# Another order for the second part of an output projection and the norms behind it, in a two-layer diffusion trunk

## The chip, the cores and the metric

The kernel runs on one core of a Trainium2 chip. The metric is device time in microseconds (us) for one execution. TensorE (PE in the profile) multiplies matrices; the loads of its stationary operand are the rows marked PEld. VectorE is DVE, ScalarE is ACT, GpSimd is POOL, and SyncE is SP, which issues the DMAs of this kernel. Every engine works through its own instructions in a fixed order.

## The reference

The reference is one inference step of a trunk with two layers. Five blocks of 128 tokens (four of latents, one of context) go through each layer. The part that the change touches is the end of the attention sub-layer and the beginning of the feed-forward one:

```python
o_s = window_attention_latent(rope_2d(q), rope_2d(k), v, ...) @ w_o_a[j]
...
xp = xp + mp[2] * op
xs = xs + ms[2] * o_s
hp = modulate(rmsnorm(xp, norm_ffn_w[i]), mp[3], mp[4])
hs = modulate(rmsnorm(xs, norm_ffn_w[i]), ms[3], ms[4])
...
u = h @ w_up          # first step of conv_ffn: 1024 x 5632
```

The attention output times `w_o` (1024 x 1024), with a gate, is added to x. Each row of x is then normalised, scaled and shifted, and becomes the input of the up-projection. The second layer does the same with `w_o_b`.

## The kernel before

Values are float32, and a product is made of three: each operand is split into a high part (rounded, in the type fp32r) and a low part (value minus high part), and high x high, high x low and low x high are summed. ACT makes the high part (L157 for weights, L389 for the normalised activations), POOL subtracts to get the low part (L160, L390). So a weight tile is a DMA into a staging tile, an ACT copy and a POOL subtraction.

Half of the output projection's sum is done during attention (`o_first`, tile `ps_op`). `finish_layer` runs the second half, once per layer, and then the feed-forward part. The words of one string give its order:

```python
OPROJ = "00 10 20 01 11 21 n0 30 n1 40 w0 n2 31 41 w1 u0 n3d w2 u1 n4d u2 u0 u1 u2"
```

- `th`, as `31`: `product` for token block t and column half h (512 columns). Four k steps, 18 matmuls into `ps_dn` (two buffers). DVE multiplies by the gate (L476, which frees the buffer) and adds to x (L477, both inputs in SBUF). With h = 1 it also starts `norm_stat`: ACT squares the row of x and sums (L352), a few small DVE and ACT steps make the reciprocal root (L299 to L306), and DVE scales the row into `xn` (L353). The weights of a column half are three pieces of 768, 768 and 512 columns.
- `nt`: `norm`: eight PE transposes of `xn` (L138, `ps_nt`), then `norm_post`: per half of four 128-blocks, scale and shift on DVE (L379, first half) or ACT (L381, second half), the high part on ACT (L389, tiles `hF_00` and `hF_01`), the low part on POOL (L390, tiles `hF_10` and `hF_11`).
- `wi`: load of an up-projection weight tile (128 columns of `w_up`) in two pieces of 768 and 256 columns. The 768 pieces, and the 256 of w0, are staged in `ust`, the other two in `wst`. High and low parts lie in six rotating pairs of buffers (`w_bufs` = 6), which the six pieces of the output projection hold before them: w0 takes the two pairs of the first column half's first pieces, w1 that half's third and the second column half's first, w2 the second half's other two. A piece can be written once the last product that reads its pair is through with it.
- `ui`: half of an up product: 320 columns, that is token blocks 0, 1 and half of 2 in the first half, the rest in the second. It has 24 matmuls; the first twelve read `hF_00` and `hF_10`, the last twelve `hF_01` and `hF_11`.

Behind these words two more up tiles are loaded ahead (`wx`, 1024 columns each, staged in a second `ust` tile that can be filled only when PE has read `oh` and `ol`, the split attention output, for the last time, in product 41).

PE's order is the order of the words (`chain` in `mm` and `tr`). On the other engines and the DMA queue a scheduler fixes the order of the instructions when the kernel is built; nothing is reordered at run time.

Of the kernel before, what the change touches and what calls it, by code (L numbers as in the profile page):

```python
# [51 lines left out]

LAST = "40a 41a 00a 01a 40b 41b 00b 01b 10 11 n4 20 n0 21 30 n1 31 n2 q6 n3"

OPROJ = "00 10 20 01 11 21 n0 30 n1 40 w0 n2 31 41 w1 u0 n3d w2 u1 n4d u2 u0 u1 u2"


def _f(ap):
# [1127 lines left out]
def finish_layer(k, l, wo, of, xsrc, cw):  # L1186
    nc = k.nc
    with ExitStack() as c:
# [39 lines left out]
        ust = k.ap.tile([P, 4 * T], F32, name="ust", tag="act")  # L1228
        for c_ in OPROJ.split():
            i = int(c_[1])  # L1230
# [158 lines left out]
```

## Time and profile before

| | |
|---|---|
| median of 3 runs | 1721.25 us (1717.64 to 1725.33) |
| profiled execution | 1718.12 us, of which the span from first to last instruction is 1716.3 us |
| PE busy | 94% of the span |
| PEld, DVE, ACT, POOL busy | 85%, 50%, 45%, 55% |
| mean granted TensorE clock | 0.981 of full speed |

PE is busy nearly all the time, so its idle times and its slow stretches are what can be won or lost. The words of `OPROJ` run from about 362 to 425 us in layer 0, and again, with the same pattern, from about 1212 to 1274 us in layer 1.

### The profile page before, as it was taken

What the parts mean: (1) busy time and instruction counts of PE and PEld (TensorE: products, weight loads), DVE (VectorE), ACT (ScalarE), POOL (GpSimd) and SP (SyncE); (2) the same over time, 40 slices, a digit from 0 to 9 for tenths busy, and PEclk for the clock granted to TensorE, in tenths of its full rate; (3) what the DMA queues carried; (4) which work ended last, traced back from release to release, by engine and by line L of the source; (5) the groups of instructions that cost most, each with busy time, mean ns of one, the idle gap of its engine ahead of it and who ended that gap; (6) DMA issues with size and microseconds to landing.
All of it is one profiled execution on the core that took longest, in us unless ns stands there. A gap on an engine that the chain in (4) does not pass through costs nothing. (4 is left out here: it accounts for less than half of the span.)

```text
span 1716.3 us, 26311 instructions
## 1 busy us (share of the span) xinstructions
PE 1619.1 (94%) x9736; PEld 1453.7 (85%) x9736; DVE 862.6 (50%) x2109; ACT 771.5 (45%) x1719; POOL 939.4 (55%) x786
## 2 busy tenths in 40 slices
PE   6789989999999999999969999998999999999998
PEld 4557767678999999999868899987899999999997
DVE  5766676765323243233555667677643333332334
ACT  4556566536323233223446777776452323323131
POOL 1434345447565675656336766776365647646461
PEclk9899999999999999999989999999999999999999
DMA  8455465561322222222122211223522212213131
GB/s 315 148 204 183 181 224 205 191 222 52 97 70 78 74 86 74 74 74 73 63 87 77 70 53 50 61 94 118 168 86 75 86 62 87 86 50 99 50 99 62
DMA packets 74592, 184.86 MB, mean 108 GB/s; under 512 B 16200, under 2 KB 25672, under 8 KB 74464
## 3 DMA queue, kind: packets, MB, share of 16 engines
q1 hardware_dynamic: 74464, 183.18, 32.0%
q8 instruction: 77, 1.26, 0.3%
q14 instruction: 51, 0.42, 0.1%
HBM read 171.32 MB, written 14.12 MB: 108 GB/s over the span
## 5 line engine op out<-in xcount | busy, mean ns | idle before, releaser
L132 PE MATMUL ps_up<-hF,whi 128*128 128x320 f32 x2688 | 598.6, 310 | 5.4 <-POOL hF L390 5.4
L160 POOL TENSOR_TENSOR wlo<-wst,whi 128x1024 fp32r<-128x1024 f32 (+3 forms) x190 | 417.1, 2199 | 218.8 <-ACT whi L157 218.5
L132 PEld LDWEIGHTS ps_up<-hF,whi 128*128 128x128 f32 x2688 | 454.8, 189 | 12.6 <-POOL hF L390 6.0
L132 PE MATMUL ps_up<-hF,wlo 128*128 128x320 f32 x1344 | 415.3, 310 | 0.0
L157 ACT ACTIVATE whi<-wst 128x1024 fp32r<-128x1024 f32 (+3 forms) x195 | 186.7, 962 | 415.1 <-PE ps_dn L132 158.0
L936 DVE SCALAR_TENSOR_TENSOR z<-ps_up,convc,z 128x511 f32<-128x511 f32 (+1 forms) x176 | 96.0, 545 | 331.1 <-ACT z L934 331.1
L132 PEld LDWEIGHTS ps_up<-hF,wlo 128*128 128x128 f32 x1344 | 253.1, 189 | 1.7
L477 POOL TENSOR_TENSOR x<-x,xtmp 128x512 f32<-128x512 f32 x100 | 128.8, 1293 | 143.1 <-DVE xtmp L476 143.0
L476 DVE TENSOR_TENSOR xtmp<-ps_dn,gate 128x512 f32<-128x512 f32 x120 | 81.9, 690 | 244.5 <-PE ps_dn L132 244.5
L132 PE MATMUL ps_mm<-whi,hB 128*128 128x384 f32 x580 | 181.3, 351 | 9.3 <-DVE rs_r L341 8.5
L132 PE MATMUL ps_dn<-whi,gh 128*128 128x512 f32 x440 | 172.8, 393 | 1.7 <-DVE xtmp L476 1.6
L132 PE MATMUL ps_dn<-wlo,gh 128*128 128x512 f32 x440 | 172.3, 392 | 0.0
L132 PE MATMUL ps_dn<-whi,gl 128*128 128x512 f32 x440 | 169.8, 389 | 0.0
L132 PE MATMUL ps_mm<-whi,hA 128*128 128x384 f32 x320 | 111.0, 376 | 8.3 <-ACT hA L268 6.3
L132 PEld LDWEIGHTS ps_mm<-whi,hB 128*128 128x128 f32 x580 | 108.7, 190 | 11.5 <-ACT vb L527 8.9
L961 POOL TENSOR_TENSOR gl<-z,gh 128x640 fp32r<-128x640 f32 x44 | 69.3, 1575 | 81.9 <-ACT gh L960 81.9
L937 DVE SCALAR_TENSOR_TENSOR z<-ps_up,convc,z 128x511 f32<-128x511 f32 (+1 forms) x176 | 96.8, 550 | 6.1
L132 PE MATMUL ps_mm<-wlo,hB 128*128 128x384 f32 x290 | 98.6, 340 | 0.0
L132 PEld LDWEIGHTS ps_dn<-whi,gh 128*128 128x128 f32 x440 | 82.6, 188 | 17.9 <-DVE xtmp L476 3.4
L934 ACT ACTIVATE z<-ps_up,convc 128x640 f32<-128x640 f32 x88 | 77.0, 875 | 45.7 <-PE ps_up L132 45.6
L132 PEld LDWEIGHTS ps_dn<-whi,gl 128*128 128x128 f32 x440 | 82.2, 188 | 17.2
L132 PEld LDWEIGHTS ps_dn<-wlo,gh 128*128 128x128 f32 x440 | 82.6, 188 | 13.6
(214 smaller groups left out, 2919.4 us busy)
## 6 DMA issues: line engine op xcount, KB each, us to landing
adst<-in_wada_dram SPq DMA_DIRECT2D x96, 512.0 KB, 6.1
wst<-in_wup_dram SPq DMA_DIRECT2D x78, 512.0 KB, 3.4
wst<-in_wdown_dram SPq DMA_DIRECT2D x44, 512.0 KB, 3.4
wst<-in_wqb_dram SPq DMA_DIRECT2D x29, 384.0 KB, 3.2
wst<-in_wqa_dram SPq DMA_DIRECT2D x16, 384.0 KB, 6.9
xd<-xring SPq DMA_DIRECT2D x20, 256.0 KB, 6.3
x<-xd SPq DMA_DIRECT2D x10, 512.0 KB, 5.6
wst<-in_woa_dram SPq DMA_DIRECT2D x8, 384.0 KB, 5.7
```

The lines of the kernel that those rows point to most:

```text
L132: i = self.nc.tensor.matmul(out, lhsT, rhs, start=start, stop=stop)
L157: i = nc.scalar.activation(hi, st, AF.Copy)
L160: (lo_eng or nc.gpsimd).tensor_tensor(lo, st, _f(hi), OP.subtract)
L476: nc.vector.tensor_tensor(tmp, ps, gate[:, j, sl], OP.mult)
L477: (nc.gpsimd if pool_add else nc.vector).tensor_tensor(x[:, sl], x[:, sl], tmp, OP.add)
L934: nc.scalar.activation(z, u, AF.Identity, scale=w[:, 1:2], bias=w[:, 3:4])
L936: nc.vector.scalar_tensor_tensor(z[:, a + 1:b], u[:, a:b - 1], w[:, 0:1], z[:, a + 1:b], op0=OP.mult, op1=OP.add)
L937: nc.vector.scalar_tensor_tensor(z[:, a:b - 1], u[:, a + 1:b], w[:, 2:3], z[:, a:b - 1], op0=OP.mult, op1=OP.add)
L961: nc.gpsimd.tensor_tensor(gl[:, k], zz[0], _f(gh[:, k]), OP.subtract)
```

## The change

One string is another. The same words stand in another order, and no instruction is added or removed.

```diff
-OPROJ = "00 10 20 01 11 21 n0 30 n1 40 w0 n2 31 41 w1 u0 n3d w2 u1 n4d u2 u0 u1 u2"
+OPROJ = "00 10 20 30 40 w0 01 11 21 n0 31 n1 41 n2 w1 u0 n3d w2 u1 n4d u2 u0 u1 u2"
```

All five first column halves come first. The first up weights w0 are loaded right behind them. Then come the second halves, with n0, n1 and n2 behind 21, 31 and 41. Before, products 31 and 41 stood between n2 and u0; now n2 stands right before u0.

On PE, at the end of the projection in layer 0, before (`oh`, `ol` are the attention output, `ps_nt` the transposes of a norm, `ps_up` the up product u0):

```order
L132 MATMUL ps_dn_4325<-whi_4006,ol_3971 128x512
L132 MATMUL ps_dn_4325<-whi_4012,oh_3970 128x512
L132 MATMUL ps_dn_4325<-wlo_4013,oh_3970 128x512
L132 MATMUL ps_dn_4325<-whi_4012,ol_3971 128x512
L132 MATMUL ps_up_4369<-hF0_00_4018,whi_4261 128x320
L132 MATMUL ps_up_4369<-hF0_10_4020,whi_4261 128x320
```

and now:

```order
L132 MATMUL ps_dn_4304<-whi_4012,oh_3970 128x512
L132 MATMUL ps_dn_4304<-wlo_4013,oh_3970 128x512
L132 MATMUL ps_dn_4304<-whi_4012,ol_3971 128x512
L138 MATMUL ps_nt_4337<-ident_72,xn_4215 128x128 x8
L132 MATMUL ps_up_4369<-hF0_00_4018,whi_4120 128x320
L132 MATMUL ps_up_4369<-hF0_10_4020,whi_4120 128x320
```

The transposes of token 2 (`xn_4215`) have moved from two products ahead of u0 to directly ahead of it.

On POOL, in the same place, before. `xn_4134` is token 1 and `xn_4167` token 2; `wlo_4262`, `wlo_4267` are w0, `wlo_4359`, `wlo_4364` w1, `wlo_4417`, `wlo_4422` w2, and `wx` the two tiles loaded ahead:

```order
L390 TENSOR_TENSOR hF0_10_4020<-xn_4134,hF0_00_4018 128x4x128
L160 TENSOR_TENSOR wlo_4262<-ust_4024,whi_4261 128x768
L160 TENSOR_TENSOR wlo_4267<-ust_4024,whi_4266 128x256
L390 TENSOR_TENSOR hF0_11_4021<-xn_4134,hF0_01_4019 128x4x128
L160 TENSOR_TENSOR wlo_4359<-ust_4024,whi_4358 128x768
L390 TENSOR_TENSOR hF0_10_4020<-xn_4167,hF0_00_4018 128x4x128
L160 TENSOR_TENSOR wlo_4364<-wst_4365,whi_4363 128x256
L390 TENSOR_TENSOR hF0_11_4021<-xn_4167,hF0_01_4019 128x4x128
L160 TENSOR_TENSOR wlo_4417<-ust_4024,whi_4416 128x768
L160 TENSOR_TENSOR wlo_4422<-wst_4423,whi_4421 128x256
L160 TENSOR_TENSOR wx_4572<-ust_4571,wx_4572 128x1024
L160 TENSOR_TENSOR wx_4576<-ust_4571,wx_4576 128x1024
```

and now, with `xn_4182` for token 1 and `xn_4215` for token 2 (w0 and the first piece of w1 stand ahead of these rows and of token 0):

```order
L160 TENSOR_TENSOR wlo_4364<-wst_4365,whi_4363 128x256
L390 TENSOR_TENSOR hF0_10_4020<-xn_4182,hF0_00_4018 128x4x128
L160 TENSOR_TENSOR wlo_4417<-ust_4024,whi_4416 128x768
L160 TENSOR_TENSOR wlo_4422<-wst_4423,whi_4421 128x256
L390 TENSOR_TENSOR hF0_11_4021<-xn_4182,hF0_01_4019 128x4x128
L160 TENSOR_TENSOR wx_4572<-ust_4571,wx_4572 128x1024
L390 TENSOR_TENSOR hF0_10_4020<-xn_4215,hF0_00_4018 128x4x128
L160 TENSOR_TENSOR wx_4576<-ust_4571,wx_4576 128x1024
L390 TENSOR_TENSOR hF0_11_4021<-xn_4215,hF0_01_4019 128x4x128
```

Both pieces of w2 and the first `wx` tile have moved from behind token 2 to ahead of its first low part, and the second `wx` tile to between its two.

On ACT, now, from the second piece of w1 on (`xn_4269` and `x_3966` are token 3):

```order
L157 ACTIVATE whi_4363<-wst_4365 128x256
L389 ACTIVATE hF0_00_4018<-xn_4182 128x4x128
L381 ACTIVATE xn_4182<-ps_nt_4283,mcol0_83,abA01_3943 128x128 x2
L352 ACTIVATE xn_4269,nss_4270<-x_3966 128x1024
L381 ACTIVATE xn_4182<-ps_nt_4283,mcol0_83,abA01_3943 128x128 x2
L157 ACTIVATE whi_4416<-ust_4024 128x768
L157 ACTIVATE whi_4421<-wst_4423 128x256
L300 ACTIVATE rs_l_4273<-rs_a_4272 128x1
L389 ACTIVATE hF0_01_4019<-xn_4182 128x4x128
L157 ACTIVATE wx_4572<-ust_4571 128x1024
L389 ACTIVATE hF0_00_4018<-xn_4215 128x4x128
```

The first of these rows writes a buffer that product 41 reads in its first two k steps, and the whole of token 1's split stands behind it; before, token 1's first high part stood three weight pieces earlier.

## Rows read from the trace of the kernel before

**Rows 1.** The page: busy us of each engine, share of the span, instructions
```profile
PE 1619.1 (94%) x9736; PEld 1453.7 (85%) x9736; DVE 862.6 (50%) x2109; ACT 771.5 (45%) x1719; POOL 939.4 (55%) x786
```

**Rows 2.** PE's waits: engine, line, releaser: us in total, times, longest; last row 415-850 us
```profile
PE ps_up L132 <- POOL hF L390: 5.4, 2, 2.7
...
PE ps_dn L132 <- DVE xtmp L476: 0.8, 1, 0.8
```

**Rows 3.** PE in order of time: start, duration, line, operation, tiles [idle before, releaser]
```profile
379.73 1.09 PE L138 MATMUL ps_nt<-ident,xn 128*128 128x128 f32 x8 [0.22 <-DVE xn L353]
...
387.14 0.40 PE L132 MATMUL ps_dn<-whi,ol 128*128 128x512 f32 x1
...
388.72 0.48 PE L132 MATMUL ps_dn<-whi,oh 128*128 128x512 f32 x1
...
394.39 0.30 PE L132 MATMUL ps_up<-hF,whi 128*128 128x320 f32 x1
397.38 0.64 PE L132 MATMUL ps_up<-hF,whi 128*128 128x320 f32 x1 [2.69 <-POOL hF L390]
...
400.48 0.56 PE L132 MATMUL ps_up<-hF,whi 128*128 128x320 f32 x2
...
402.34 1.03 PE L138 MATMUL ps_nt<-ident,xn 128*128 128x128 f32 x8
```

**Rows 4.** Windows: stretch, us, busy time of each engine, granted clock, DMA share, GB/s
```profile
397.40:400.50 3.10, 3.10 (x12) 3.10 (x13) 2.25 (x6) 2.42 (x6) 3.10 (x3) 0.50 0.37 152
```

**Rows 5.** POOL in order of time, layer 0, from the first norm on
```profile
383.21 1.49 POOL L390 TENSOR_TENSOR hF<-xn,hF 128x512 fp32r<-128x512 f32 x1 [10.66 <-ACT hF L389]
...
389.58 2.56 POOL L160 TENSOR_TENSOR wlo<-ust,whi 128x768 fp32r<-128x768 f32 x2 [0.64 <-ACT whi L157]
392.09 1.32 POOL L390 TENSOR_TENSOR hF<-xn,hF 128x512 fp32r<-128x512 f32 x1
...
395.61 1.72 POOL L390 TENSOR_TENSOR hF<-xn,hF 128x512 fp32r<-128x512 f32 x1
397.28 0.73 POOL L160 TENSOR_TENSOR wlo<-wst,whi 128x256 fp32r<-128x256 f32 x1
397.97 1.28 POOL L390 TENSOR_TENSOR hF<-xn,hF 128x512 fp32r<-128x512 f32 x1
399.21 2.28 POOL L160 TENSOR_TENSOR wlo<-ust,whi 128x768 fp32r<-128x768 f32 x1
...
402.59 4.75 POOL L160 TENSOR_TENSOR wx<-ust,wx 128x1024 fp32r<-128x1024 f32 x2
```

**Rows 6.** ACT in order of time, layer 0, around product 41
```profile
391.47 1.51 ACT L381 ACTIVATE xn<-ps_nt,mcol,abA 128x128 f32<-128x128 f32 x4
392.89 0.42 ACT L157 ACTIVATE whi<-wst 128x256 fp32r<-128x256 f32 x1
393.21 0.61 ACT L389 ACTIVATE hF<-xn 128x512 fp32r<-128x512 f32 x1
394.03 1.06 ACT L352 ACTIVATE xn<-x 128x1024 f32<-128x1024 f32 x1 [0.20 <-issue]
...
395.09 0.83 ACT L157 ACTIVATE whi<-ust 128x768 fp32r<-128x768 f32 x1
...
397.99 1.06 ACT L157 ACTIVATE wx<-ust 128x1024 fp32r<-128x1024 f32 x1 [0.47 <-DMA ust<-in_wup_dram]
```

**Rows 7.** DVE in order of time, layer 0: additions to x
```profile
366.38 0.69 DVE L477 TENSOR_TENSOR x<-x,xtmp 128x512 f32<-128x512 f32 x1
...
388.44 1.05 DVE L477 TENSOR_TENSOR x<-x,xtmp 128x512 f32<-128x512 f32 x1
...
392.54 1.42 DVE L477 TENSOR_TENSOR x<-x,xtmp 128x512 f32<-128x512 f32 x1
```

**Rows 8.** DMA issues (SP queue) in order of time: the last load of x, layer 0
```profile
369.93 0.32 SPq L1203 DMA_DIRECT2D x<-xd  x1
```

**Rows 9.** The page, DMA issues: tiles, count, KB each, median us to landing
```profile
x<-xd SPq DMA_DIRECT2D x10, 512.0 KB, 5.6
```

## The prediction

> **What bounds the kernel.** Read the busy times first: PE is busy for 1619.1 us, 94% of the span [rows 1], so a change of order can only win or lose PE's idle times and its slow stretches. Then read PE's waits. In the stretch of the change the wait of an up product for POOL stands out: 5.4 us, once per layer, 2.7 each [rows 2]. PE's instructions in order of time show it. u0's first matmul follows the last product at 394.39, and its second starts only at 397.38, when POOL has written the first low part of token 2 [rows 3]. The windows show a second price: 12 matmuls take the 3.10 us from 397.40 on, at a granted clock of 0.50, which is 1.2 of 2.4 GHz, right after that wait [rows 4]. At full clock 12 take 1.86 (400.48 to 402.34) [rows 3]. So u0's first half lasts from 394.39 to 402.34, 7.95 us, where 24 matmuls at full clock need 3.72: a loss of 4.23 us per layer, of 2.99 waiting and 1.24 clock. That is what a better order could win here, about 8.5 in two layers. Behind u0 PE has a single wait of 0.8 up to 850 us [rows 2], so time lost at u0 isn't caught up later: it is added to the end.
>
> The third view is POOL in order of time. It gets to token 2's first low part at 395.61 because two pieces of w0 (2.56) and the first of w1 lie ahead of it; w2 (2.28 for its first piece, which is as large as w1's) and the two tiles loaded ahead (4.75) come behind it [rows 5]. So the question is what lies between n2 and u0 on POOL after the change, and the rows of the new order answer it.
>
> **The change, part by part,** for layer 0; T is the time at which the last product ends (394.39 before).
>
> *The n2 slot.* n2's transposes leave the row of products. From the start of 40's last matmul plus one spacing (387.14 + 0.23) to 31's first (388.72) they took 1.35 us [rows 3]; T comes earlier by that, and the transposes run inside the wait that follows. Gain 1.35.
>
> *ACT.* The high part of w1's second piece writes a buffer that product 41 reads in its first two k steps. Before, it ran at 392.89, 1.50 ahead of T [rows 6]. In the new row token 1's split, token 3's square and w2's first piece stand behind it. The piece, one high part, the square and the 768 piece ran from 392.89 to 395.92, which is 3.03; the four scale steps add 1.42 (391.47 to 392.89) [rows 6]. So w2's first high part is ready at T - 1.50 + 4.45 = T + 2.95. The bounds are T + 2.0, if the buffer comes free a microsecond earlier, and T + 4, if ACT also waits for DVE's half of token 1.
>
> *POOL.* From there it has w2's first piece 2.28, the second 0.73, token 1's second part 1.28, a `wx` tile 2.38 (half of 4.75), and only then token 2's first part, 1.28 [rows 5]: 7.95 in all. u0's second matmul can start at T + 10.9, where it was T + 2.99. The second `wx` tile and token 2's second part follow, 3.66, so the thirteenth matmul can't start before T + 14.55.
>
> *u0.* After so long without work I take the first 12 matmuls at the half clock, 3.10 [rows 4], to T + 14.0. They then wait 0.55 for the second part, and 12 at full clock end at T + 16.4. Before, it was T + 7.95. The loss is 8.45, less the slot's 1.35: 7.1 us.
>
> *Earlier weights.* w0 and w1's first piece (2.56 and about 2.28 us of POOL, 4.84) now run under the products 01 and 11, where POOL stood idle: it waited 10.66 ahead of 383.21 [rows 5]. They cost nothing there, except through DVE. An addition to x alone takes 0.69; the one at 392.54 beside POOL took 1.42 [rows 7]. It ended at 393.96, 0.55 after the POOL instruction of 392.09 [rows 5]. Now 40's and 01's additions meet these pieces, and 01's starts the chain of token 0's norm, for which PE already waits 0.22 [rows 3]. An addition 0.73 later moves n0 by less, since the norm's next DVE step is queued behind the next product's gate: I take 0.4, between 0 and 2.3 (a whole piece). The Trainium skill (SBUF — State Buffer, "Who interferes with whom") says that a DVE instruction with two SBUF inputs and a GpSimd instruction that reads SBUF exclude each other, and that the later one waits for the whole of the other. The rows agree. By the rule at its worst, 01's addition waits out a whole 2.3 us piece: 1.9 more per layer, and a time of 1740 in place of the one below.
>
> *DMAs.* Four loads into `ust` now come ahead of the last loads of x. The last was issued at 369.93 [rows 8] and its first addition was at 388.44 [rows 7]. Now product 40 comes three products (2.83 each, half of 388.72 to 394.39 [rows 3]) and two norms (1.35 each) earlier, so it adds at about 377.2, 7.3 after that issue, where a load takes 5.6 [rows 9]. I take 0, with an upper bound of 1 us. The second `ust` is still loaded at T; before, ACT copied from it 3.6 us after T (397.99) [rows 6]. Now ACT gets there at about T + 4.2 and POOL at T + 7.2, so 0.
>
> *Everything behind u0* stands in the old order: n3, u1, n4, u2. Their inputs have the same distances or longer ones. Cost 0; it is covered by u1 and u2, and if tokens 3 and 4 came late, u0's second half would wait.
>
> **Sum.** 7.1 + 0.4 = 7.5 us per layer. Layer 1 has the same words, the same new rows on POOL, and the same wait before [rows 2]: 15 in all. Against the profiled execution of 1718.1 that gives 1733.1. The median of the runs shown is 3.1 above it; 15 on the median, 1721.25, gives **1736**. Bounds per layer: about 5.5 (ACT a microsecond earlier, no DVE loss, half of the second part's delay hidden) and 11 (ACT a microsecond later, the second 12 matmuls at half clock too for 1.24, a DVE loss of 1.5): 1732 to 1743.
>
> **Rivals.**
>
> 1. *POOL is free in time, and it isn't slower.* If token 2's first part found POOL idle, only n2's own chain would show. From n0's transposes at 379.73 to the end of its first low part at 384.70 took 4.97 [rows 3, 5]. u0's second matmul would start at T + 5.0, not T + 2.99; less the 1.35 that is + 0.65 per layer: 1722.5. The earlier weights speak for it, since 4.84 us leave POOL's way; the order speaks against it, which puts w2 and a `wx` tile, 5.4 us, in the way instead. It decides whether that low part begins by T + 3.7.
> 2. *A gain.* Were u0 not to wait at all, 8.5 would be won: 1712.8. But 4.97 us from n2 to its low part is longer than the 2.99 that PE waited, so this needs a shorter norm chain than any row shows.
> 3. *Clock and contention add up.* If all 24 matmuls of u0 run at 1.2 GHz and DVE and POOL hold each other up twice more, 10 to 11 per layer: 1742. For it: PE would be idle about three times as long as before. Against: the clock came back within 3.1 us of work.
> 4. *The change acts in one layer only*: + 7.5, 1728.8. The rows of both layers are the same, so this is nearly ruled out.
>
> **How the numbers follow.** A measurement of this kernel can tell about 0.5%, 8.6 us, from no change. The forecast (0.73) and rival 3 (0.13) are slower by more than that: 0.86. Rivals 1 (0.08) and 4 (0.03) lie within it: 0.11. Rival 2 has 0.03. The range of 1727 to 1743 holds the forecast's bounds, with a few microseconds below for the spread of the runs, and the lower half of rival 3; it leaves out rivals 1 and 2.
>
> **What would show it.** In the profile after, PE should wait at `ps_up` for POOL twice in each layer, about 9 to 10 us first and up to 2 at the thirteenth matmul, in place of 2.7 once; POOL's low part of token 2 should start 9 to 10 us after the last product; and the granted clock should be 0.50 for about 3 us from there. The products before should run without gaps, but for about 0.6 at n0. If the low part comes within 5 us of T, the forecast is wrong at the ACT or POOL step; if PE's waits are as said and the time isn't longer, it is wrong in that lost time adds to the end.

## The result and the profile after

The changed kernel takes 1735.14 us (median of 6 runs, 1732.97 to 1739.72), the kernel before 1719.45 on the same chip (6 runs, 1716.58 to 1725.33): 15.7 us more, a ratio of 1.0087 with a 95% interval of 1.0070 to 1.0104. The forecast was 15 more, 1736.

The profiled execution of the change took 1739.72. Its first product starts at 368.7, where it is 362.6 in the one of before. Up to there the instructions are the same, and of the change nothing but the first loads of up weights has been issued: the 6.1 us are spread between executions (in the fourteen profiles of this document that product starts anywhere from 360.4 to 368.7). So stretches are compared here, and not whole spans. I take the stretch of the words from PE's first product (`ps_dn`) to its first matmul with a tile loaded ahead (`wx`). PE's instructions by tile (count, duration in ns, first and last start), layer 0, before:

```profile
L132 PE MATMUL ps_dn<-whi,oh x50: 277/389/496, 362.6 to 393.7; 128*128 128x512 f32 x30, 128*128 128x256 f32 x20
L132 PE MATMUL ps_up<-hF,wx x96: 309/309/309, 421.8 to 435.7; 128*128 128x320 f32 x96
```

and after:

```profile
L132 PE MATMUL ps_dn<-whi,oh x50: 277/389/504, 368.7 to 398.3; 128*128 128x512 f32 x30, 128*128 128x256 f32 x20
L132 PE MATMUL ps_up<-hF,wx x96: 309/309/309, 435.4 to 449.4; 128*128 128x320 f32 x96
```

The words take 59.2 before and 66.7 after: 7.5 more. In layer 1 they take 59.1 (1211.8 to 1270.9) and 66.5 (1225.8 to 1292.3): 7.4 more. From layer 0's words to layer 1's it is 790.0 and 790.4. So 14.9 of the 15.7 lie where the change was made, in both layers.

The page, busy us and instructions, for [rows 1]:

```profile
PE 1625.7 (94%) x9736; PEld 1458.9 (84%) x9736; DVE 865.9 (50%) x2109; ACT 771.8 (44%) x1719; POOL 937.8 (54%) x786
```

PE's 6.6 us more of busy time say little of the change: the instructions are the same, 3.8 of the 6.6 lie ahead of the first product, and only 1.7 in the two stretches of the words. PE's waits, for [rows 2]; the last line is that of 415 to 870 us:

```profile
PE ps_up L132 <- POOL hF L390: 10.2, 4, 4.8
PE ps_up L132 <- ACT hF L389: 8.1, 2, 4.2
PE ps_nt L138 <- DVE xn L353: 7.4, 5, 3.4
...
PE ps_dn L132 <- DVE xtmp L476: 0.8, 1, 0.8
```

5.4 of waiting at `ps_up` have become 18.3. `xn` waits stand as before (7.2 there), and the later stretch has the same single wait of 0.8. PE in order of time, for [rows 3]:

```profile
391.42 1.09 PE L138 MATMUL ps_nt<-ident,xn 128*128 128x128 f32 x8 [0.21 <-DVE xn L353]
...
398.81 0.39 PE L132 MATMUL ps_dn<-whi,ol 128*128 128x512 f32 x1
399.71 1.10 PE L138 MATMUL ps_nt<-ident,xn 128*128 128x128 f32 x8 [0.52 <-DVE xn L353]
404.66 0.64 PE L132 MATMUL ps_up<-hF,whi 128*128 128x320 f32 x1 [3.85 <-ACT hF L389]
410.11 0.63 PE L132 MATMUL ps_up<-hF,whi 128*128 128x320 f32 x1 [4.81 <-POOL hF L390]
...
413.20 0.47 PE L132 MATMUL ps_up<-hF,whi 128*128 128x320 f32 x1
414.12 0.56 PE L132 MATMUL ps_up<-hF,whi 128*128 128x320 f32 x1 [0.45 <-POOL hF L390]
...
415.98 1.03 PE L138 MATMUL ps_nt<-ident,xn 128*128 128x128 f32 x8
```

T, the end of the last product, is 398.81 + 0.23 = 399.04. From the second matmul of u0 (410.11) to the thirteenth (413.20) it is 3.10 us. The window of these matmuls, for [rows 4], has a clock of 0.50 again:

```profile
410.10:413.20 3.10, 3.09 (x11) 3.10 (x12) 2.72 (x2) 0.00 (x0) 3.10 (x2) 0.50 0.00 0
```

POOL, for [rows 5]: w0 and w1's first piece early, then w2, token 1's second part, a `wx` tile, token 2's first part, the other `wx` tile and token 2's second part.

```profile
382.14 4.80 POOL L160 TENSOR_TENSOR wlo<-ust,whi 128x768 fp32r<-128x768 f32 x3 [0.67 <-ACT whi L157]
...
402.36 1.81 POOL L160 TENSOR_TENSOR wlo<-ust,whi 128x768 fp32r<-128x768 f32 x1 [1.55 <-ACT whi L157]
...
404.80 1.28 POOL L390 TENSOR_TENSOR hF<-xn,hF 128x512 fp32r<-128x512 f32 x1
406.02 2.36 POOL L160 TENSOR_TENSOR wx<-ust,wx 128x1024 fp32r<-128x1024 f32 x1
408.33 1.72 POOL L390 TENSOR_TENSOR hF<-xn,hF 128x512 fp32r<-128x512 f32 x1
410.01 2.36 POOL L160 TENSOR_TENSOR wx<-ust,wx 128x1024 fp32r<-128x1024 f32 x1
412.34 1.73 POOL L390 TENSOR_TENSOR hF<-xn,hF 128x512 fp32r<-128x512 f32 x1
```

ACT, for [rows 6]: w2's first high part, and token 2's first one, which u0's first matmul reads:

```profile
401.38 0.84 ACT L157 ACTIVATE whi<-ust 128x768 fp32r<-128x768 f32 x1
...
403.98 0.63 ACT L389 ACTIVATE hF<-xn 128x512 fp32r<-128x512 f32 x1
```

DVE, for [rows 7]: the additions of products 40 and 01, beside POOL's early weights (382.14 to 386.94), are longer, as forecast, but by 0.4 at most, and the one that follows them has the 0.69 of an undisturbed one:

```profile
383.63 0.90 DVE L477 TENSOR_TENSOR x<-x,xtmp 128x512 f32<-128x512 f32 x1
...
386.41 1.08 DVE L477 TENSOR_TENSOR x<-x,xtmp 128x512 f32<-128x512 f32 x1
...
389.19 0.69 DVE L477 TENSOR_TENSOR x<-x,xtmp 128x512 f32<-128x512 f32 x1
```

The last load of x, for [rows 8], is issued at 378.81, and the fifth addition is at 383.63: a margin of 4.8, not the 7.3 of the forecast, because the load is now issued 10.1 behind the first product, where it was 7.3 [rows 8]. No wait shows there.

### The profile page after: what moved, and what is told of

Same layout as the page of the kernel before. It is cut to its first block, busy times and chain, and to the rows that moved or that the text cites. A ratio compares the mean times of both kernels' runs of the same rounds, so it can differ in the third digit from the quotient of the medians.

```text
span 1737.6 us, 26308 instructions
## 1 busy us (share of the span) xinstructions
PE 1625.7 (94%) x9736; PEld 1458.9 (84%) x9736; DVE 865.9 (50%) x2109; ACT 771.8 (44%) x1719; POOL 937.8 (54%) x786
## 5 line engine op out<-in xcount | busy, mean ns | idle before, releaser
L132 PE MATMUL ps_up<-hF,whi 128*128 128x320 f32 x2688 | 600.1, 310 | 18.3 <-POOL hF L390 10.2
L132 PEld LDWEIGHTS ps_up<-hF,whi 128*128 128x128 f32 x2688 | 455.1, 189 | 26.7 <-POOL hF L390 11.7
L132 PEld LDWEIGHTS ps_dn<-wlo,gh 128*128 128x128 f32 x440 | 82.7, 188 | 13.6
```

The lines of the kernel that those rows point to most:

```text
L132: i = self.nc.tensor.matmul(out, lhsT, rhs, start=start, stop=stop)
```

## The experiments

Three helpers serve them. `lo_eng=nc.vector` makes a low part on DVE. `pin_lo` puts a low part's subtraction behind the instruction that stands before it in the program on its engine. `after` puts a weight's high and low part behind two given instructions of ACT and POOL, in the queue alone and without a wait. `post[t]` are token t's last high and low part, `stat[t]` is its reciprocal root's last step on ACT (L303). The cuts of code show the lines that use them; those that define them and hand them on are left out, and `...` marks a place left out between two lines.

All results in one table: words of each layer; both layers together against before; the time between the layers' words (790.0 before); the median against that of before on the same chip; the ratio's interval.

| run | words 0 | words 1 | both | between | median | interval |
|---|---|---|---|---|---|---|
| before | 59.2 | 59.1 | | 790.0 | | |
| the change | 66.7 | 66.5 | +14.9 | 790.4 | +15.7 | 1.0070 to 1.0104 |
| e1_pool_order | 65.2 | 66.1 | +13.0 | 789.5 | +13.1 | 1.0065 to 1.0098 |
| e2_wx_behind | 63.0 | 63.6 | +8.3 | 792.1 | +9.2 | 1.0039 to 1.0076 |
| e3_n2_earlier | 61.3 | 64.8 | +7.8 | 792.0 | +8.6 | 1.0040 to 1.0070 |
| e4_before_pool_order | 63.2 | 62.8 | +7.7 | 790.7 | +9.8 | 1.0046 to 1.0076 |
| e5_t2_low_on_dve | 67.2 | 67.2 | +16.1 | 789.4 | +16.9 | 1.0089 to 1.0115 |
| e6_before_w1_on_dve | 58.5 | 58.3 | -1.5 | 791.7 | +0.8 | 1.0001 to 1.0018 |
| e7_before_t2_low_on_dve | 63.3 | 63.2 | +8.2 | 786.7 | +5.6 | 1.0029 to 1.0058 |
| e8_before_w1_behind_t2 | 59.2 | 59.0 | -0.1 | 788.3 | +0.7 | 0.9989 to 1.0011 |
| e9_t2_first_everywhere | 61.9 | 61.9 | +5.5 | 791.3 | +5.9 | 1.0034 to 1.0069 |
| e10_before_chains_first | 56.2 | 56.1 | -6.0 | 790.2 | -6.2 | 0.9953 to 0.9977 |
| e11_late_w0 | 73.7 | 73.8 | +29.2 | 789.5 | +29.3 | 1.0136 to 1.0199 |
| e12_before_wx_and_w1_behind | 60.3 | 60.0 | +2.0 | 792.3 | +5.3 | 1.0015 to 1.0040 |

The time between the words moves by -3.3 to +2.3 in runs where the build put the second layer's attention in another order (e2, e3, e6, e7, e9 and e12 among them). Part of that is spread: in e8, whose order there is nearly that of before, it moved by -1.7. The verdicts below go by the words.

**What stands ahead of token 2 on POOL.**

```diff
-            k.norm_post(k.norm_tr(xn, t, dn=where == "d"), xn, l, 1, t, hT)
+            k.norm_post(k.norm_tr(xn, t, dn=where == "d"), xn, l, 1, t, hT, pin=False, pin_lo=t == 2)
...
-                ups.append(k.up(hT, [k.load_w(src[:, a:b], b - a, k.wp, None, s)
+                ups.append(k.up(hT, [k.load_w(src[:, a:b], b - a, k.wp, None, s, False, i == 2)
...
-                                  ust[:, 1024 * i:1024 * i + 1024]))
+                                  ust[:, 1024 * i:1024 * i + 1024], False, True))
```

The last argument of `load_w` is `pin_lo`.

> The changed kernel with POOL's order alone altered: both low parts of token 2 stand ahead of w2 and of the two wx tiles, directly behind token 1's second low part. PE's, DVE's and SP's order in these places stays, ACT's but for one square. T is the end of the last product. Theory (what is queued on POOL ahead of token 2 makes the loss): token 2's first high part is ready at about T + 5.6 as in the changed kernel, so its low part ends at about T + 6.9 and u0's second matmul starts there instead of at T + 11.1. Twelve matmuls at half clock end at T + 10.1, the second low part is done by about T + 9.9, and u0's first half ends at about T + 11.9 instead of T + 16.9: 5 us less per layer, 10 in all, about 1725. Rival 1 (n2's own chain directly ahead of u0 is the loss and POOL stands by): PE waits for ACT instead and the time stays between 1732 and 1736. Rival 2 (the loss comes from the column order and the early weights, which hold up DVE): the same, 1732 to 1736, with later starts of n0 to n2.

PE in order of time in this run, layer 0:

```profile
402.39 0.63 PE L132 MATMUL ps_up<-hF,whi 128*128 128x320 f32 x1 [0.93 <-POOL hF L390]
406.38 0.64 PE L132 MATMUL ps_up<-hF,whi 128*128 128x320 f32 x1 [0.42 <-POOL hF L390]
408.93 1.04 PE L138 MATMUL ps_nt<-ident,xn 128*128 128x128 f32 x8
...
416.46 0.42 PE L132 MATMUL ps_up<-hF,wlo 128*128 128x320 f32 x1 [1.80 <-POOL wlo L160]
```

POOL's wait fell from 4.81 to 0.93, as forecast, but u2 then waited 1.80 for w2, which the pin had put behind token 3 as well. u0's first half won 3.4 in layer 0, where 5 were expected, since it also waited 0.42 for token 2's second low part and went on at the lower clock behind that. The words kept 1.5, and 0.4 in layer 1. So the expectation failed by what is late next.

The second run drops the pin on w2:

```diff
-                ups.append(k.up(hT, [k.load_w(src[:, a:b], b - a, k.wp, None, s, False, i == 2)
+                ups.append(k.up(hT, [k.load_w(src[:, a:b], b - a, k.wp, None, s)
```

> The changed kernel with the POOL subtractions of the two wx tiles behind token 2's low parts; w2 stays ahead of them. Theory: token 2's first low part follows token 1's second one at about T + 7.0, and u0's second matmul starts at T + 8.4 instead of T + 11.1; no wait at the thirteenth; u0's first half ends at T + 13.4: 3.5 us less per layer, 7 in all, about 1728. Together with the run in which w2 goes behind too this gives the shares of wx and w2. Rivals 1 and 2: 1732 to 1736. The build also puts ACT's and DVE's instructions of the second layer's attention in another order, which may move the total by some microseconds; layer 0 is read from its own rows.

```profile
405.36 0.63 PE L132 MATMUL ps_up<-hF,whi 128*128 128x320 f32 x1 [2.06 <-POOL hF L390]
```

3.7 and 2.9 us less than the change, where 3.5 were expected, without a new wait: the two `wx` tiles are wanted only behind the words, and their place ahead of token 2 was 39 to 49% of the loss.

**n2's place.**

```diff
-OPROJ = "00 10 20 30 40 w0 01 11 21 n0 31 n1 41 n2 w1 u0 n3d w2 u1 n4d u2 u0 u1 u2"
+OPROJ = "00 10 20 30 40 w0 01 11 21 n0 31 n1 n2 41 w1 u0 n3d w2 u1 n4d u2 u0 u1 u2"
```

> The changed kernel with n2 one product earlier, ahead of product 41: first column halves first and w0 early, as in the change, but a product between n2 and u0. Theory: token 2's low part is now second on POOL only to token 1's; n2 waits up to 1.5 for its norm, u0's second matmul waits 1 to 2.5, and about half of the first twelve matmuls run at half clock: near the time of the kernel before, 1716 to 1724. Rival 1 (n2's place is the loss) says the same, so the run of POOL's order decides between these two. Rival 2 (column order and early weights are the loss): 1730 to 1736, since both are still there.

```profile
396.52 1.97 PE L138 MATMUL ps_nt<-ident,xn 128*128 128x128 f32 x8 [3.15 <-DVE xn L353]
```

u0's first half no longer waits in layer 0, but n2 does, 3.15 for its own norm, and its transposes run at the lower clock (1.97 against 1.09). u0's second half waits 0.88. In layer 1 u0 waits 2.60 and n4 1.55 besides n2. The time lies between the two expectations. The column order and the early weights alone don't cost the 14.9 (against rival 2), but n2's wait was put at half of what it is: n0, 31 and n1 between 21 and n2 are shorter than its chain by 3 us.

**Early weights, undone.**

```diff
-OPROJ = "00 10 20 30 40 w0 01 11 21 n0 31 n1 41 n2 w1 u0 n3d w2 u1 n4d u2 u0 u1 u2"
+OPROJ = "00 10 20 30 40 01 11 21 n0 31 n1 w0 41 n2 w1 u0 n3d w2 u1 n4d u2 u0 u1 u2"
```

> The changed kernel with one part undone: w0 is loaded late again (behind n1 instead of behind the first column halves); the column order and n2's place stay. The prediction took the early weights at no cost, and as 4.84 us that leave POOL's way. Theory: these pieces now stand on ACT (2.5 us) and POOL (w0 2.56 and w1's first piece 2.28) between token 1 and token 2. POOL runs w0, w1, token 1's second half and w2 in a row from about T + 2.5 on, so token 2's first low part ends at about T + 13.6 instead of T + 11; its second one, behind both wx tiles, at T + 19.7 instead of T + 15.1. u0's first half ends at T + 21.6 to T + 22.8 instead of T + 16.9: 4.7 to 5.9 more per layer, 1744 to 1747. Rival (the early weights help nothing, or cost DVE what they save POOL): within 2 per layer of the changed kernel, 1731 to 1739.

```profile
401.44 0.63 PE L132 MATMUL ps_up<-hF,whi 128*128 128x320 f32 x1 [5.15 <-ACT hF L389]
408.29 0.64 PE L132 MATMUL ps_up<-hF,whi 128*128 128x320 f32 x1 [6.22 <-POOL hF L390]
414.58 0.64 PE L132 MATMUL ps_up<-hF,whi 128*128 128x320 f32 x1 [2.73 <-POOL hF L390]
```

7.0 and 7.3 more per layer than the change, above the 4.7 to 5.9 expected. The second matmul came where it was expected (at T + 13.6), but the rest of u0's first half and n3's transposes then ran at the lower clock (0.50 in the windows 408.3 to 411.4 and 414.6 to 417.7). So the change has two parts of opposite sign: the column order with n2 at the end costs 14.5 and 14.7 per layer, and the early weights give 7 of it back.

**DVE instead of POOL.** Token 2's low parts on DVE, in the change (e5) and in the kernel before (e7); w1's in the kernel before (e6):

```diff
-            k.norm_post(k.norm_tr(xn, t, dn=where == "d"), xn, l, 1, t, hT)
+            k.norm_post(k.norm_tr(xn, t, dn=where == "d"), xn, l, 1, t, hT, lo_eng=nc.vector if t == 2 else None)
...
-                ups.append(k.up(hT, [k.load_w(src[:, a:b], b - a, k.wp, None, s)
+                ups.append(k.up(hT, [k.load_w(src[:, a:b], b - a, k.wp, nc.vector if i == 1 else None, s)
```

> The changed kernel with both low parts of token 2 made by DVE instead of POOL; w2 and the wx tiles keep their places on POOL, so nothing is pushed behind. Theory (token 2's low part lost its time in POOL's queue, and the run of POOL's order gave the gain back because w2 then came 2 us too late for u2): the high part is ready at T + 5.6, DVE makes the low part by T + 6.5 to T + 8, u0's first half ends at T + 11.5 to T + 13 instead of T + 16.9, and there is no wait for w2. DVE's two more instructions delay tokens 3 and 4 by up to 1.5. Gain 3 to 5 per layer: 1725 to 1729. Rival (in this stretch any order pays the same, since the sum of the work bounds it): 1732 to 1736.

DVE in order of time in e5:

```profile
398.73 0.76 DVE L390 TENSOR_TENSOR hF<-xn,hF 128x512 fp32r<-128x512 f32 x1 [1.95 <-ACT hF L389]
...
401.04 2.48 DVE L353 TENSOR_SCALAR xn<-x,rs_r 128x1024 f32<-128x1024 f32 x1
403.44 2.82 DVE L390 TENSOR_TENSOR hF<-xn,hF 128x512 fp32r<-128x512 f32 x1
```

and POOL:

```profile
400.58 5.13 POOL L160 TENSOR_TENSOR wx<-ust,wx 128x1024 fp32r<-128x1024 f32 x2
```

PE's first wait for a low part fell to 0.25: that part came in time, but the second one stood behind token 3's scaling, and both were held while POOL split the `wx` tiles: 2.82 for what takes 0.76 alone. PE waited 3.24 at the fourteenth matmul and ran all of u0's first half and n3's transposes at a clock of 0.50. The words take 0.5 and 0.7 more than in the change: nothing of the 3 to 5 per layer was won.

> The kernel before with the low parts of w1 made by DVE. On POOL token 2's low parts then follow token 1's second one directly. Theory: u0's second matmul waits 0.3 to 0.5 instead of 2.7 and at full clock: 3.1 to 4 less per layer, as in the run of the kernel before with POOL's order altered; w1 and w2 are early, so u1 and u2 don't wait. DVE has 1.5 us more to do ahead of the last additions to x, and POOL may hold it up: n3 and n4 wait 1.2 to 2.5. Net gain 1 to 2.5 per layer: 1715 to 1718. Rival (what POOL gives up DVE pays in full, n3 later by as much as u0 is earlier): 1719 to 1722.

> The kernel before with token 2's low parts made by DVE. They stand on DVE behind the gates of the last two products and ahead of additions to x. Theory: u0's second matmul starts within 0.5 of its first, 4 less per layer; token 3's addition comes 0.7 to 1.5 later, so n3 waits 1.5 to 2.5: net 1.5 to 2.5 per layer, 1715 to 1718. Rival: n3 and n4 wait 4 in all, 1720 and more. The build also orders the second layer's attention anew, which cost 2 us in two runs that had the same.

In e6 u0's wait fell to 1.17, and n3 then waited 1.41 and n4 0.49. The words won 0.7 and 0.8 per layer, and the stretch between them, whose attention the build had put in another order, was 1.7 longer (791.7); the net is the rival's. In e7 u0 waited 1.04, at its fourteenth matmul, but n3 5.66:

```profile
406.61 1.94 PE L138 MATMUL ps_nt<-ident,xn 128*128 128x128 f32 x8 [5.66 <-DVE xn L353]
```

Both expectations were too high by what tokens 3 and 4 lose.

**POOL's order in the kernel before.** The pins of e1, with `pin_lo=i >= 1` on the weights (e4) or `i == 1` (e8), and none on `wx`:

> The kernel before with POOL's order alone altered: both low parts of token 2 ahead of w1's first piece (and w2 behind token 3). Theory: token 2's first high part is ready at 391.6 in the trace of before, so its low part can run from 393.35, when token 1's second ends, to 394.7; u0's second matmul starts 0.3 after its first instead of 2.99, at full clock, and the second low part ends before the thirteenth. Of the 4.23 per layer about 4 are won, 8 in all: about 1711.5. Rival: the clock falls at u0 whether PE waits or not, or w1 then comes late for u1: only 2.7 or less per layer, 1714 to 1719.

```profile
413.47 0.63 PE L132 MATMUL ps_up<-hF,wlo 128*128 128x320 f32 x1 [2.74 <-POOL wlo L160]
```

u0's wait fell to 0.45, and its first half ended 3.7 earlier; n3 waited 1.22, and u2 waited 2.74 for w2, with the lower clock behind it. 4.0 and 3.7 more per layer in all: the pins had put w2 behind token 3 again.

> The kernel before with one exchange on POOL: w1's first piece goes behind token 2's two low parts, and nothing else (w2 and the wx tiles keep their places; ACT and SP are the same). It is the run of POOL's order on the kernel before without the 2.7 us wait for w2 and the half clock behind it, which cost 6 there. Theory: u0 3.1 earlier, n3 1.2 and n4 0.5 later, as seen there: 1.4 less per layer, 3 in all, about 1717. Rival (what is put behind always comes late: w1 for u1): u1 waits for wlo for 1 to 3, no gain, 1720 to 1725.

PE in order of time in e8:

```profile
393.05 0.41 PE L132 MATMUL ps_up<-hF,whi 128*128 128x320 f32 x1 [0.47 <-POOL hF L390]
...
397.90 1.06 PE L138 MATMUL ps_nt<-ident,xn 128*128 128x128 f32 x8 [1.21 <-DVE xn L353]
...
403.11 1.09 PE L138 MATMUL ps_nt<-ident,xn 128*128 128x128 f32 x8 [0.63 <-DVE xn L353]
...
409.08 0.42 PE L132 MATMUL ps_up<-hF,whi 128*128 128x320 f32 x1 [1.21 <-POOL hF L390]
```

This is the cleanest exchange, and the most telling: u0's first half ends 3.7 us earlier (T + 4.25 in place of T + 7.95), and n3, n4 and u0's second half give back all of it, 1.4 at n3 and 2.3 behind it. (w1's second piece, which the expectation doesn't name, went behind token 2's second low part with the first one.) u1 doesn't wait, so the rival's reason was wrong and its time right. ACT shows why n3 is late:

```profile
391.93 1.06 ACT L352 ACTIVATE xn<-x 128x1024 f32<-128x1024 f32 x1 [0.21 <-issue]
...
392.98 0.83 ACT L157 ACTIVATE whi<-ust 128x768 fp32r<-128x768 f32 x1
...
394.88 1.06 ACT L352 ACTIVATE xn<-x 128x1024 f32<-128x1024 f32 x1 [0.67 <-POOL hF L390]
...
395.94 0.19 ACT L303 ACTIVATE rs_l<-rs_l 128x1 f32<-128x1 f32 x1
```

Between token 3's square (391.93) and the end of its root (395.94) stand w2 and token 4's square. The row names POOL for the square's wait, but POOL's part had ended at 394.26; what ended at 394.80 is token 4's addition to x, which took DVE 1.60 beside POOL and not 0.69.

**The norms first, on ACT and on POOL.** These are for the kernel before in e10 and e12 (e12 is e10 without `stat[3]`), and for the change in e9, whose edit is:

```diff
-                ups.append(k.up(hT, [k.load_w(src[:, a:b], b - a, k.wp, None, s)
+                ups.append(k.up(hT, [k.load_w(src[:, a:b], b - a, k.wp, None, s, after=post[2] if i == 2 else ())
...
-                                  ust[:, 1024 * i:1024 * i + 1024]))
+                                  ust[:, 1024 * i:1024 * i + 1024], after=post[2]))
```

and in e10:

```diff
-                ups.append(k.up(hT, [k.load_w(src[:, a:b], b - a, k.wp, None, s)
+                ups.append(k.up(hT, [k.load_w(src[:, a:b], b - a, k.wp, None, s, after=((), (None, post[2][1]), (stat[3],))[i] if i else ())
...
-                                  ust[:, 1024 * i:1024 * i + 1024]))
+                                  ust[:, 1024 * i:1024 * i + 1024], after=post[4]))
```

> The changed kernel with token 2 first on both engines: w2's and the wx tiles' high parts on ACT behind token 2's two high parts, their low parts on POOL behind its two low parts; w2 follows at once, ahead of tokens 3 and 4. No word of the order moves. Theory (the loss is what the build queued ahead of token 2 on ACT and then POOL; the runs so far took only POOL's part away and paid for it with a late w2 or a late second low part): only n2's own chain is left. The first high part is ready at about T + 3.9, the first low part at T + 5.3, u0's second matmul starts there instead of at T + 11.1, twelve at half clock end at T + 8.4, u0's first half at about T + 10.4 instead of T + 16.9. w2's low part is done at about T + 10, u2 wants it at T + 17. Gain 6.5 per layer: what is left over the kernel before is 1 per layer, 1721 to 1724. This is also the measure of rival 1 of the prediction (POOL free in time, 1722.5). Rival (in this stretch the work is only moved about: what goes behind token 2 comes late again): a wait of 2 or more at u1 or u2, gain under 3 per layer, 1728 to 1734.

```profile
398.05 0.64 PE L132 MATMUL ps_up<-hF,whi 128*128 128x320 f32 x1 [2.59 <-ACT hF L389]
400.21 0.64 PE L132 MATMUL ps_up<-hF,whi 128*128 128x320 f32 x1 [1.53 <-POOL hF L390]
```

4.8 and 4.6 of the 7.5 and 7.4 are won back, none given up later. That is less than the 6.5 expected and more than the rival's 3: token 2's first low part still runs behind token 1's second one, and behind the wait 17 matmuls, and not 11, run at a clock of 0.50 (4.70 us from 400.2 on). 2.7 and 2.8 per layer remain: with no weight between token 1's and token 2's parts, this order of words still loses that against the kernel before. No product stands between n2 and u0 to cover the chain; that this is the reason is argued, and no run of it was made.

> The kernel before with three things put behind the chain of the norms: on POOL w1 behind token 2's low parts (as in the run that exchanged these two alone and won 3.4 at u0, and gave back 1.0 at n3, 0.8 at n4 and 1.4 at u0's second half), and the wx tiles behind token 4's; on ACT w2's high parts behind token 3's reciprocal root, and the wx tiles' behind token 4's high parts. Theory: the three waits that took the gain back are token 3's and 4's norms standing on ACT behind w2 and on POOL behind wx; without these n3 waits under 0.4, n4 and u0's second half under 0.5: 2.5 to 3.3 less per layer than before, 1713 to 1716. Rival (DVE, which POOL holds up, sets n3 and n4): n3 still waits 1 or more, 1717 to 1720.

```profile
395.26 0.42 PE L132 MATMUL ps_up<-hF,whi 128*128 128x320 f32 x1 [0.46 <-POOL hF L390]
399.43 1.06 PE L138 MATMUL ps_nt<-ident,xn 128*128 128x128 f32 x8 [0.53 <-DVE rs_a L299]
403.85 1.03 PE L138 MATMUL ps_nt<-ident,xn 128*128 128x128 f32 x8
```

3.0 less than before in each layer, and 1715.44 against 1721.59, an interval below 1: the version that beats both kernels. u0 keeps what e8 won, and the three waits behind it are gone but for 0.53.

> The run that won on the kernel before, less its edit of ACT: w1 behind token 2's low parts on POOL and the wx tiles behind token 4's, on POOL and on ACT, but w2's high parts stand on ACT where they stood, ahead of token 3's reciprocal root. It divides the 3.0 per layer. Theory: u0's second half no longer waits for token 4's low part (1.4 back), and n4 waits less, but n3 still waits about 1.2 for its norm: 1.5 to 2.2 per layer, 1716 to 1718.5. Rival 1 (ACT's order doesn't matter): 3 per layer, 1714 to 1716. Rival 2 (it is ACT's order alone): no gain, 1719 to 1722. The build orders the second layer's attention anew, which gave between -3 and +2 us in other runs; the layers' own stretches are read apart from it.

```profile
403.42 1.61 PE L138 MATMUL ps_nt<-ident,xn 128*128 128x128 f32 x8 [2.96 <-DVE rs_r L306]
```

n3 waited 2.96, and the words took 1.1 and 0.9 more than before. That is nearest to rival 2: one queue place on ACT (w2 behind token 3's root) is worth 4 us per layer here (e10 against e12), and the `wx` tiles' place alone wins nothing (e12 is 1 slower than e8). Token 4's square stood ahead of the end of token 3's root again, and the scaling behind it met w2's subtraction on POOL:

```profile
400.99 2.28 DVE L353 TENSOR_SCALAR xn<-x,rs_r 128x1024 f32<-128x1024 f32 x1
```

That scaling took 0.77 in e8 and 1.54 in e10. So 0.7 of the 4 come from a longer meeting with POOL, and not from ACT's order as such.

## Why the prediction was right

Its sum is 7.1 + 0.4 per layer, and 7.5 and 7.4 were measured. Step by step:

- **The n2 slot and DVE.** From the first product to T it is 31.8 before (394.39 - 362.6) and 30.3 after: 1.5 earlier. The slot's 1.35 is all there; the 0.4 for DVE is not: n0's gap is 0.21 where it was 0.22. A whole piece of 2.3, the upper bound, was never waited for: 01's addition took 1.08.
- **ACT.** w2's first high part at T + 2.95; it is ready at 402.22, T + 3.2.
- **POOL.** 7.95 to the end of token 2's first low part; 7.69 from 402.36 to 410.05. u0's second matmul at T + 10.9; it is at T + 11.1. But the wait is in two pieces: 3.85 for ACT's high part and then 4.81 for POOL. I named POOL alone; the high part stood behind w2 on ACT too.
- **The clock.** From the second matmul to the thirteenth it took 3.10, as forecast. The prediction misread one thing here: eleven matmuls start in that time, before and after, and not twelve, so the lower clock costs 1.4 and the wait itself 2.84 of the 4.23. The sum isn't touched, since it used the 3.10 as a whole. The next wait came at the fourteenth matmul, the first that reads the second low part, at T + 15.1 and not T + 14.55. Most of that is POOL's start, T + 3.3 for T + 2.95; its pieces took 11.7 for 11.6, token 2's two parts being longer (1.72 and 1.73 for 1.28) and w2's first one shorter (1.81 for 2.28). u0's first half ends at T + 16.9, 0.5 later than forecast. That and the absent 0.4 cancel, so the agreement to a tenth is luck; the path and its large terms are not.
- **Behind u0** the profile shows no new wait; the time lost was added to the end, as forecast. From n3's transposes to the first matmul with a `wx` tile it is 19.4 in both kernels.

Three sentences around the sum were wrong, and a forecast of another change would have failed on them. "That is what a better order could win here", of the 4.23 at u0: e8 won 3.7 of it and not a microsecond in all. n3, n4 and u0's second half stood just behind, covered by u0's wait, and the trace of before could not show waits that another wait hides. The early weights were put at no cost, but what they gave was under-sized: 4.84 of POOL, where e11 measures 7. Late, they also stand in ACT's way (u0's first matmul starts at T + 6.8 for T + 5.6), and the second low part and the clock add the rest. And rival 1 (+0.65 with POOL free) would have been 2.7, as e9 shows. It left out that token 1's second half stands ahead of token 2 on both engines (u0's second matmul starts at T + 6.5 for its T + 5.0), and that the slow stretch then was longer (17 matmuls for 11, 0.6 more to the end of u0's first half).

Rivals 2, 3 and 4 did not come. Nothing was won. Among the products POOL held DVE's additions up by 0.5 at most, without a wait of PE; the long holds came behind them, at the scaling of tokens 3 and 4 (1.99 and 2.61 for 0.75), and u0's wait covered them. And both layers lost the same. Which of ACT's and DVE's steps make up e9's remaining 2.7 wasn't tried further, nor was e10's queue order together with the early weights.

## What to carry to other kernels

Cost a new order by walking each in-order queue from the last free moment to the item that the bottleneck waits for: here that put the end of u0's first half, 17 us behind the last product, right to 0.5 us. Before crediting a removed wait, ask which chains it covers and how late each would be without it; the gain is the distance to the next late one. And where a program word moves, look at what the build queues ahead of the critical item on every engine it passes: here the old order of words, with two queues put right, won 3.0 per layer.

## What the runs showed of the hardware

A scaling of one SBUF row tile by a column, L353, is held up by POOL like the additions with two inputs: 0.75 alone, 2.28 (e12), 2.48 (e5) and 2.84 (e8) where a split on POOL had begun just before it. The profile books this as busy time of the held instruction, not as a wait, so a long duration is the sign. The Trainium skill (SBUF — State Buffer, "Who interferes with whom") says that the later of the two fully blocks until the other's instruction ends. The rows agree: L390's 2.82 in e5 ends at 406.26 with POOL done at 405.71, and L353's 2.28 in e12 at 403.27 with POOL's piece done at 402.72, both 0.55 behind it.

Behind waits of 0.46 (e10) and 1.21 (e8), ahead of u0 and n3, the granted clock of the next matmuls was 1.00, the level of 2.4 GHz. Behind those of 2.69 [rows 3], 3.15 (e3) and 3.85 + 4.81 (the change) it was 0.50, the level of 1.2 GHz. So each of these short waits cost itself alone, and the long one of 2.69 another 1.4 us: 3.10 for eleven matmuls that take 1.7 at full clock.
